# Low half of the second down weight tile of each feed-forward group: a VectorE subtraction in place of an accumulating DMA

## The chip, the cores and the metric

The kernel runs on one core of a Trainium2 chip. The metric is the device time of one execution in microseconds. The median of three runs before the change is 1435.9 us (1432.58 to 1439.35).

## The reference

One step of a hybrid decoder trunk of one layer, for a prompt of 1024 tokens and 8 sample sequences of 4 tokens that share the weights. What matters here is the second half of the layer:

```
h = x * (1 + scale2) + shift2
u = causal depthwise conv width 3 of (h @ w_up);  f = (silu(u_a) * u_b) @ w_down
x = LayerNorm(ALPHA * x + gate2 * f)
```

with `D_MODEL` 1024 and `D_FF` 2816, all in float32. Ahead of it stand the modulation, a combined projection, differential attention, a convolution branch, the output projection and a first LayerNorm.

## The kernel before

All 1056 tokens lie along the free dimension, in three chunks of 352 (`CH`). Features lie on the partitions. A float32 product is made of three matmuls in a 32-bit format of fewer bits (fp32r): each operand is split into a high half (a cast) and a low half (what the cast left), and `mm3` (lines 173 to 178) adds high x high (L176), high x low input (L177) and low weight x high input (L178) in PSUM.

**Weights.** They come as tiles of 128 x 1024 in the order of the list `wsrc` (lines 126 to 142). `prefetch_w` (lines 152 to 165) takes the next entry: SP loads it into `wst` (two buffers), ScalarE casts it into `whi` (L159), and the low half `wlo` is made in one of two ways, by the entry's second field `how`. With `"dma"`, ScalarE writes -hi into `wlo` (L161) and POOL issues a DMA that adds `wst` onto it in place (L162). With an engine, that engine subtracts (L164). `whi` and `wlo` have three buffers each, so a tile's cast waits until the matmuls of the tile three places earlier have ended.

**The feed-forward stage.** The 22 blocks of 128 features are worked off in groups of `FG` = 2, groups 0 to 10. A group has six weight tiles, in this order: for its first feature block the tiles of the two halves of `w_up` (called u1a, u1b here), the same for the second (u2a, u2b), then two tiles of `w_down` (d1, d2). For each block and chunk, `Up.chunk` (lines 1055 to 1086) makes two products into PSUM banks (`psb`, four in turn); ScalarE copies each out (L1062, L1063, L1065 for the sample columns of the last chunk), VectorE does the convolution taps (L1068, L1072), then SILU (L1078), the product (L1079), and the split into `ah` (L1080, ScalarE) and `al` (L1082, POOL). `down` (lines 1088 to 1094) then runs, chunk by chunk, eight blocks of six matmuls each: three with d1, three with d2. VectorE adds each block into the accumulator `acc` (L1179), which empties the bank.

Groups 1 to 9 make all low halves with `"dma"`; group 0 with VectorE. In group 10 the list `LAST` (line 44) sets the order: up and down for chunks 0 and 1 with `"dma"`, then the last chunk, whose tiles are loaded once more, with VectorE. `norm2` (lines 1096 to 1143) normalizes each chunk in three row tiles: statistics (L1116), a Newton iteration (L245 to L247), a scaling copy on ScalarE (L1134), an accumulating DMA of the bias (L1135) and the store (L1143), with four buffers `y`.

The order of instructions on each engine is set by a scheduler that runs its own timeline of the program, so that a change in one place can reorder others.

Of the kernel before, what the change touches and what calls it, by code (L numbers as in the profile page):

```python
# [36 lines left out]
FG = 2  # L37
# [31 lines left out]
def body(tc, nc, io):  # L69
    ex = ExitStack()  # L70
    with ex:
# [58 lines left out]
        for f0 in range(0, KF, FG):  # L130
            once = nc.vector if f0 // FG == CHUNK_OUTER[0] else "dma"

            def blocks(what, how):
                return [(io["w_up"][m], how) for f in range(f0, f0 + FG) for m in (f, KF + f)] if what == "u" else \
                    [(io["w_down"][f], how) for f in range(f0, f0 + FG)]

            if f0 + FG == KF:
                for w, cs in LAST:
                    if w != "n":
                        wsrc += blocks(w, "dma" if len(cs) > 1 else nc.vector)  # L140
            else:
                wsrc += blocks("u", once) * (NCH if f0 // FG in CHUNK_OUTER else 1) + blocks("d", once)
# [277 lines left out]
        with tc.tile_pool(name="pa", bufs=2, reuse_waits="tile") as pa:  # L420
# [19 lines left out]
            def flip_x(c):  # L440
                n = 4 if c < EARLY else 1
                for d0 in range(0, KD, n):
# [6 lines left out]
                    for j in range(n):  # L449
                        nc.scalar.copy(xs[c][:, d0 + j, :], ps[j][:, 0, :CH])  # L450

            blocks, loaded = [w + d for d in range(KD) for w in (0, 8)], []

            def load_ada():
# [830 lines left out]
```

## Time and profile before

| | us |
|---|---|
| median of the runs | 1435.9 (1432.58 to 1439.35) |
| the profiled execution | 1439.02 |
| its span | 1437.3 |
| busy: TensorE (PE) | 1356.3 |
| busy: VectorE (DVE) | 899.7 |
| busy: ScalarE (ACT) | 643.2 |
| busy: GpSimd (POOL) | 338.6 |
| mean granted TensorE clock, as a share | 0.975 |

Busy times are sums over one execution, taken by the hardware profiler. Matmuls are pipelined: one is recorded with some 0.32 us, the next starts 0.16 us after it, so a busy PE need not be at its peak. A line such as L178 is the line of the kernel that issued the instruction. "Idle before" is the time in which an engine stood still ahead of an instruction, with what ended it.

### The profile page before, as it was taken

The page shows a single profiled execution, that of the slowest core. Times are in us where ns is not written, and L with a number is a line of the kernel's source. Part 1 is how long each engine was busy: PE and PEld are TensorE (multiplying, and loading weights), DVE is VectorE, ACT ScalarE, POOL GpSimd, SP SyncE. Part 2 cuts the span into 40 slices and gives each one's busy share as a digit, 9 for nine tenths or more (in the row PEclk, how much of TensorE's full clock was granted, in tenths as well). Part 3 has the DMA queues.
Part 4 walks back from the last instruction along what each step waited for, and adds up shares of the span by engine and source line. Part 5 has one row for each costly group of instructions (what it writes and reads, how often), then busy time and mean ns, then how long its engine had stood idle before and what let it go on. Part 6 is the DMA issues. An engine that isn't in the chain of part 4 may idle for free.

```text
span 1437.3 us, 24575 instructions
## 1 busy us (share of the span) xinstructions
PE 1356.3 (94%) x9449; PEld 1271.1 (88%) x9449; DVE 899.7 (63%) x1954; ACT 643.2 (45%) x1170; POOL 338.6 (24%) x454
## 2 busy tenths in 40 slices
PE   7899999999999899789999999999999999999983
PEld 6798999996666798779999999999999999999983
DVE  5759999437777569987453545453536353535486
ACT  6542222457666455563434343435253525353532
POOL 2431110321101452324222122222222222221111
PEclk9999999999999999989999999999999999999996
DMA  9877666547764355432434243434242525252718
GB/s 302 283 214 218 185 186 192 148 130 272 239 224 166 115 173 166 123 97 76 100 78 105 72 88 90 93 84 105 72 113 65 118 60 117 59 118 60 190 57 208
DMA packets 71671, 199.68 MB, mean 139 GB/s; under 512 B 16002, under 2 KB 16514, under 8 KB 70658
## 3 DMA queue, kind: packets, MB, share of 16 engines
q1 hardware_dynamic: 57874, 145.55, 30.4%
q0 software_dynamic: 13680, 52.57, 18.8%
q8 instruction: 74, 1.21, 0.3%
q14 instruction: 43, 0.35, 0.1%
HBM read 137.49 MB, written 15.51 MB: 106 GB/s over the span
## 4 chain that ended last, share of the span: by engine, by line
PE 71%; DVE 10%; DMA 9%; issue 5%; ACT 3%; POOL 1%; SPq 0%; DVEq 0%; POOLq 0%; ACTq 0%
PE psb L176 20%; PE psb L178 20%; PE psb L177 19%; DMA wlo<-wst 6%; PE psa L836 4%; PE psb L877 2%; DVE wlo L164 2%; PE psa L319 1%; PE psb L753 1%; PE psb L866 1%; PE psb L788 1%; DMA y<-y 1%; DVE acc L1179 1%; DMA wada<-w_ada 1%; DVE t L1068 1%
## 5 line engine op out<-in xcount | busy, mean ns | idle before, releaser
L176 PE MATMUL psb<-h2h,whi 128*128 128x352 f32 x1056 | 343.1, 326 | 3.9 <-ACT h2h L294 3.9
L177 PE MATMUL psb<-h2l,whi 128*128 128x352 f32 x1056 | 341.1, 323 | 2.5 <-DVE h2l L295 2.5
L1068 DVE SCALAR_TENSOR_TENSOR t<-up,prm,t 128x352 f32<-128x352 f32 (+1 forms) x264 | 165.2, 627 | 282.9 <-ACT t L1063 280.0
L178 PE MATMUL psb<-h2h,wlo 128*128 128x352 f32 x1056 | 340.0, 325 | 0.6 <-DMA wlo<-wst 0.6
L159 ACT CAST whi<-wst 128x1024 fp32r<-128x1024 f32 x124 | 128.9, 1048 | 321.0 <-PE psb L177 283.3
L1179 DVE SCALAR_TENSOR_TENSOR acc<-psb,mod,acc 128x352 f32<-128x352 f32 (+1 forms) x288 | 160.4, 571 | 72.6 <-PE psb L178 66.7
L177 PEld LDWEIGHTS psb<-h2l,whi 128*128 128x128 f32 x1056 | 200.8, 190 | 3.3 <-DVE h2l L295 3.0
L176 PEld LDWEIGHTS psb<-h2h,whi 128*128 128x128 f32 x1056 | 199.7, 189 | 4.6 <-ACT h2h L294 4.2
L178 PEld LDWEIGHTS psb<-h2h,wlo 128*128 128x128 f32 x1056 | 199.7, 190 | 1.2 <-DMA wlo<-wst 1.2
L178 PE MATMUL psb<-ah,wlo 128*128 128x352 f32 x528 | 167.5, 327 | 8.9 <-DMA wlo<-wst 8.9
L176 PE MATMUL psb<-ah,whi 128*128 128x352 f32 x528 | 172.5, 329 | 2.7 <-DVE acc L1179 2.0
L177 PE MATMUL psb<-al,whi 128*128 128x352 f32 x528 | 172.0, 326 | 0.0
L178 PE MATMUL psb<-hh,wlo 128*128 128x352 f32 x480 | 157.0, 327 | 3.1 <-DMA wlo<-wst 3.1
L176 PE MATMUL psb<-hh,whi 128*128 128x352 f32 x480 | 158.1, 336 | 1.5 <-ACT sig L399 1.5
L177 PE MATMUL psb<-hl,whi 128*128 128x352 f32 x480 | 156.0, 326 | 0.0
L162 POOL DMA_DIRECT2D wlo<-wst x80 | 71.4, 893 | 343.3 <-ACT wlo L161 314.6
L375 DVE SCALAR_TENSOR_TENSOR cv<-u,prm,cv 128x1024 f32<-128x1024 f32 x120 | 151.3, 1296 | 0.8
L1082 POOL TENSOR_TENSOR al<-g,ah 128x352 fp32r<-128x352 f32 x60 | 60.6, 1010 | 251.8 <-ACT ah L1080 251.8
L178 PEld LDWEIGHTS psb<-ah,wlo 128*128 128x128 f32 x528 | 98.9, 190 | 11.8 <-DMA wlo<-wst 11.8
L176 PEld LDWEIGHTS psb<-ah,whi 128*128 128x128 f32 x528 | 100.2, 190 | 6.3 <-DVE acc L1179 5.0
L177 PEld LDWEIGHTS psb<-al,whi 128*128 128x128 f32 x528 | 100.5, 190 | 0.0
L1062 ACT COPY up<-psb 128x352 f32<-128x352 f32 (+1 forms) x132 | 58.4, 442 | 88.1 <-PE psb L178 88.0
(253 smaller groups left out, 2269.7 us busy)
## 6 DMA issues: line engine op xcount, KB each, us to landing
wlo<-wst POOLq DMA_DIRECT2D x80, 512.0 KB, 5.4
wst<-w_up SPq DMA_DIRECT2D x56, 512.0 KB, 3.7
wada<-w_ada SPq DMA_DIRECT2D x48, 512.0 KB, 5.3
kv<-kc SPq DMA_DIRECT2D x64, 256.0 KB, 5.4
kv<-vc SPq DMA_DIRECT2D x64, 256.0 KB, 4.6
wst<-w_out SPq DMA_DIRECT2D x24, 512.0 KB, 3.6
wst<-w_down SPq DMA_DIRECT2D x24, 512.0 KB, 4.2
wst<-w_in SPq DMA_DIRECT2D x20, 512.0 KB, 3.7
```

The costliest lines, as they stand in the source:

```text
L159: last_w["hi"] = nc.scalar.copy(hi, st)
L162: last_w["lo"] = nc.gpsimd.dma_start(lo.bitcast(F32), st, accum_op=ALU.add)
L164: last_w["lo"] = how.tensor_tensor(lo, st, hi.bitcast(F32), op=ALU.subtract)
L176: nc.tensor.matmul(ps, lhsT=wh, rhs=xh, start=start and i == 0, stop=False)
L177: nc.tensor.matmul(ps, lhsT=wh, rhs=xl, start=False, stop=False)
L178: nc.tensor.matmul(ps, lhsT=wl, rhs=xh, start=False, stop=stop and i == n - 1)
L375: nc.vector.scalar_tensor_tensor(acc, src, wj, acc, op0=ALU.mult, op1=ALU.add)
L836: nc.tensor.matmul(ps[m][:, i, :w], lhsT=q[r], rhs=k[r, i * w:(i + 1) * w], start=True, stop=True)
L1062: nc.scalar.copy(up[:, 2 + o:2 + o + npc], ps[:, 0, :npc])
L1068: nc.vector.scalar_tensor_tensor(t[:, :npc], up[:, o + j:o + j + npc], w, t[:, :npc], op0=ALU.mult, op1=ALU.add)
L1082: eng.tensor_tensor(self.al[:, c, :], g, self.ah[:, c, :].bitcast(F32), op=ALU.subtract)
L1179: nc.vector.scalar_tensor_tensor(x[:, :npc], ps[:, :npc], gate[:, 0:1], x[:, :npc], op0=ALU.mult, op1=ALU.add)
```

## The change

In every group, entries of `w_down` other than the group's first get `nc.vector` as their `how`.

```diff
             def blocks(what, how):
                 return [(io["w_up"][m], how) for f in range(f0, f0 + FG) for m in (f, KF + f)] if what == "u" else \
-                    [(io["w_down"][f], how) for f in range(f0, f0 + FG)]
+                    [(io["w_down"][f], how if f == f0 else nc.vector) for f in range(f0, f0 + FG)]
```

Ten tiles change: d2 of the groups 1 to 9, and d2 of group 10 for chunks 0 and 1. Group 0 and the last chunk had VectorE already. Each of the ten loses L161 on ScalarE and L162 on POOL's queue and gets L164 on VectorE. The scheduler moves other instructions with it.

The first place is TensorE at the start of a down phase (group 2; the other nine have the same pattern). `ah_8517` and `whi_8757` belong to the first feature block and d1, `ah_8527`, `whi_8969` and `wlo_8970` to the second and d2; `psb_8981`, `_8989`, `_8997`, `_9005` are the first four banks. Before, the rows of the fourth bank and what follows:

```order
L176 MATMUL psb_9005<-ah_8517,whi_8757 128x352
L177 MATMUL psb_9005<-al_8518,whi_8757 128x352
L178 MATMUL psb_9005<-ah_8517,wlo_8758 128x352
L176 MATMUL psb_9005<-ah_8527,whi_8969 128x352
L177 MATMUL psb_9005<-al_8528,whi_8969 128x352
L178 MATMUL psb_8981<-ah_8527,wlo_8970 128x352
L178 MATMUL psb_8989<-ah_8527,wlo_8970 128x352
L178 MATMUL psb_8997<-ah_8527,wlo_8970 128x352
L178 MATMUL psb_9005<-ah_8527,wlo_8970 128x352
L176 MATMUL psb_9013<-ah_8517,whi_8757 128x352
```

After the change, the first twelve rows of that phase (names are numbered anew; `wlo_8969` is d2's low half, `psb_8979` the first bank):

```order
L176 MATMUL psb_8979<-ah_8516,whi_8756 128x352
L177 MATMUL psb_8979<-al_8517,whi_8756 128x352
L178 MATMUL psb_8979<-ah_8516,wlo_8757 128x352
L176 MATMUL psb_8979<-ah_8526,whi_8968 128x352
L177 MATMUL psb_8979<-al_8527,whi_8968 128x352
L176 MATMUL psb_8987<-ah_8516,whi_8756 128x352
L177 MATMUL psb_8987<-al_8517,whi_8756 128x352
L178 MATMUL psb_8987<-ah_8516,wlo_8757 128x352
L176 MATMUL psb_8987<-ah_8526,whi_8968 128x352
L177 MATMUL psb_8987<-al_8527,whi_8968 128x352
L176 MATMUL psb_8995<-ah_8516,whi_8756 128x352
L178 MATMUL psb_8979<-ah_8526,wlo_8969 128x352
```

Before, the matmuls on d2's low half stood behind the 20 others of the first four banks. Now the first of them is the twelfth of the phase.

The second place is ScalarE and VectorE ahead of the same phase. ScalarE before, in group 2, from the cast of d2 (`whi_8969`) on; `psb_8892` is u2a's last product, `psb_8925` u2b's, `whi_8976` the next group's u1a:

```order
L159 CAST whi_8969<-wst_8967 128x1024
L1062 COPY up0_8519<-psb_8892 128x320
L1063 ACTIVATE t0_8917<-psb_8892,prm_73 128x352
L1065 COPY us0_8520<-psb_8892 128x8x4
L161 ACTIVATE wlo_8970<-whi_8969 128x1024
L1078 ACTIVATE g_8958<-t0_8917 128x352
L159 CAST whi_8976<-wst_8974 128x1024
L1062 COPY up1_8523<-psb_8925 128x320
```

ScalarE after:

```order
L159 CAST whi_8968<-wst_8966 128x1024
L1062 COPY up0_8518<-psb_8891 128x320
L1063 ACTIVATE t0_8916<-psb_8891,prm_73 128x352
L1065 COPY us0_8519<-psb_8891 128x8x4
L159 CAST whi_8974<-wst_8972 128x1024
L1078 ACTIVATE g_8957<-t0_8916 128x352
L1062 COPY up1_8522<-psb_8924 128x320
L1063 ACTIVATE t1_8949<-psb_8924,prm_73 128x352
```

VectorE in the same place of group 1, as a piece of the difference (`t_8229` is u2a's, `t_8262` u2b's last chunk):

```order
 L1079 TENSOR_TENSOR g<-g,t_8194 128x352
+L164 TENSOR_TENSOR wlo<-wst,whi 128x1024
 L1068 SCALAR_TENSOR_TENSOR t_8229<-up_7831,prm,t_8229 128x320
 L1072 SCALAR_TENSOR_TENSOR t_8229<-us_7832,prm,t_8229 128x32
 L1068 SCALAR_TENSOR_TENSOR t_8229<-up_7831,prm,t_8229 128x320
 L1072 SCALAR_TENSOR_TENSOR t_8229<-us_7832,prm,t_8229 128x32
+L1179 SCALAR_TENSOR_TENSOR acc_6133<-psb,mod,acc_6133 128x352 x2
 L1068 SCALAR_TENSOR_TENSOR t_8262<-up_7835,prm,t_8262 128x320
 L1072 SCALAR_TENSOR_TENSOR t_8262<-us_7836,prm,t_8262 128x32
+L1179 SCALAR_TENSOR_TENSOR acc_6133<-psb,mod,acc_6133 128x352
```

The negated copy is gone, the next group's first cast has moved ahead of the SILU, the subtraction stands ahead of u2a's last convolution step, and residual adds have come in ahead of and between u2b's convolution steps.

The third place is VectorE in the tail, where the reciprocal deviations of the first chunk's three row tiles are made (`nmt_14474`, `_14507`, `_14540` before; `nmt_14464`, `_14497`, `_14530` after). Before:

```order
L1079 TENSOR_TENSOR g_14734<-g_14734,t1_14726 128x352
L247 SCALAR_TENSOR_TENSOR nmt_14540<-nmt_14540 128x1
L245 SCALAR_TENSOR_TENSOR nmt_14507<-nmt_14507 128x1
L246 TENSOR_TENSOR nmt_14474<-nmt_14474 128x1
L1116 BN_STATS bn_14804<-psa_14793 128x6 x2
L245 SCALAR_TENSOR_TENSOR nmt_14540<-nmt_14540 128x1
L246 TENSOR_TENSOR nmt_14507<-nmt_14507 128x1
L247 SCALAR_TENSOR_TENSOR nmt_14474<-nmt_14474 128x1
L1082 TENSOR_TENSOR al_14032<-g_14734,ah_14031 128x352
```

After:

```order
L1079 TENSOR_TENSOR g_14724<-g_14724,t1_14716 128x352
L247 SCALAR_TENSOR_TENSOR nmt_14530<-nmt_14530 128x1
L246 TENSOR_TENSOR nmt_14464<-nmt_14464 128x1
L245 SCALAR_TENSOR_TENSOR nmt_14497<-nmt_14497 128x1
L245 SCALAR_TENSOR_TENSOR nmt_14530<-nmt_14530 128x1
L247 SCALAR_TENSOR_TENSOR nmt_14464<-nmt_14464 128x1
L246 TENSOR_TENSOR nmt_14497<-nmt_14497 128x1
L1116 BN_STATS bn_14794<-psa_14783 128x6
L246 TENSOR_TENSOR nmt_14530<-nmt_14530 128x1
L1116 BN_STATS bn_14794<-psa_14783 128x6
```

The last step of the first row tile (L247 on `nmt_14474`, now `nmt_14464`) stood behind the statistics of a later tile (L1116) and now stands ahead of them. On SP's queue the store of the fourth row tile now stands ahead of the third's.

## Rows read from the trace of the kernel before

**Rows 1.** The page, part 1: busy us, share of the span, instructions
```profile
PE 1356.3 (94%) x9449; PEld 1271.1 (88%) x9449; DVE 899.7 (63%) x1954; ACT 643.2 (45%) x1170; POOL 338.6 (24%) x454
```

**Rows 2.** The page, part 5: groups; busy, mean ns | idle before, what ended it
```profile
L178 PE MATMUL psb<-ah,wlo 128*128 128x352 f32 x528 | 167.5, 327 | 8.9 <-DMA wlo<-wst 8.9
L176 PE MATMUL psb<-ah,whi 128*128 128x352 f32 x528 | 172.5, 329 | 2.7 <-DVE acc L1179 2.0
```

**Rows 3.** Timeline, PE, group 5: start, us, instruction, [idle before <- releaser]
```profile
1018.58 0.32 PE L176 MATMUL psb<-ah,whi 128*128 128x352 f32 x1
...
1021.63 0.32 PE L177 MATMUL psb<-al,whi 128*128 128x352 f32 x1
1022.63 0.91 PE L178 MATMUL psb<-ah,wlo 128*128 128x352 f32 x4 [0.67 <-DMA wlo<-wst]
1023.74 0.43 PE L176 MATMUL psb<-ah,whi 128*128 128x352 f32 x1 [0.20 <-DVE acc L1179]
1024.01 0.32 PE L177 MATMUL psb<-al,whi 128*128 128x352 f32 x1
```

**Rows 4.** Timeline of the other engines around it, same columns
```profile
1014.56 0.95 POOL L1082 TENSOR_TENSOR al<-g,ah 128x352 fp32r<-128x352 f32 x1 [4.26 <-ACT ah L1080]
...
1014.77 1.05 ACT L159 CAST whi<-wst 128x1024 fp32r<-128x1024 f32 x1 [0.29 <-PE psb L177]
...
1016.65 1.08 ACT L161 ACTIVATE wlo<-whi 128x1024 fp32r<-128x1024 f32 x1
...
1016.73 0.55 DVE L1068 SCALAR_TENSOR_TENSOR t<-up,prm,t 128x320 f32<-128x320 f32 x1 [2.76 <-ACT t L1063]
...
1018.03 0.90 POOL L162 DMA_DIRECT2D wlo<-wst  x1 [0.63 <-DVE t L1068]
...
1018.18 0.50 ACT L1078 ACTIVATE g<-t 128x352 f32<-128x352 f32 x1 [0.45 <-DVE t L1072]
...
1018.61 1.05 ACT L159 CAST whi<-wst 128x1024 fp32r<-128x1024 f32 x1
...
1020.42 0.19 ACT L1065 COPY us<-psb 128x32 f32<-128x32 f32 x1
```

**Rows 5.** Timeline, PE: the waits of groups 1, 2 and 10, same columns
```profile
736.38 0.91 PE L178 MATMUL psb<-ah,wlo 128*128 128x352 f32 x4 [0.95 <-DMA wlo<-wst]
...
803.79 0.32 PE L176 MATMUL psb<-ah,whi 128*128 128x352 f32 x1
...
809.02 0.91 PE L178 MATMUL psb<-ah,wlo 128*128 128x352 f32 x4 [1.85 <-DMA wlo<-wst]
810.13 0.43 PE L176 MATMUL psb<-ah,whi 128*128 128x352 f32 x1 [0.20 <-DVE acc L1179]
...
1361.88 0.91 PE L178 MATMUL psb<-ah,wlo 128*128 128x352 f32 x4 [1.20 <-DMA wlo<-wst]
```

**Rows 6.** Windows: us, busy of PE, PEld, DVE, ACT, POOL, PEclk, DMA, GB/s
```profile
809.00:815.00 6.00, 5.79 (x25) 5.50 (x26) 3.79 (x8) 0.49 (x1) 0.94 (x1) 0.72 0.91 234
```

**Rows 7.** Line 164 on DVE: duration min/median/max in ns, first and last start
```profile
L164 DVE TENSOR_TENSOR wlo<-wst,whi x36: 1209/1220/1497, 524.1 to 1393.1; 128x1024 fp32r<-128x1024 f32 x36
```

**Rows 8.** The tail: timeline; DMA busy tenths from 1404 us; DMA issues, KB, landing
```profile
1401.10 1.30 DVE L1116 BATCH_NORM_STATS2 bn<-psa 128x6 f32<-128x512 f32 x2
...
1420.16 1.41 DVE L1131 SCALAR_TENSOR_TENSOR y<-psa,nmv,gb 128x512 f32<-128x512 f32 x2 [2.90 <-DMA y<-y]
...
1402.62 2.19 ACT L1134 ACTIVATE y<-y,nmt 128x1024 f32<-128x1024 f32 x2 [1.36 <-DVE nmt L247]
...
1404.07 0.89 POOL L1135 DMA_DIRECT2D y<-gb  x1 [9.00 <-ACT y L1134]
...
DMA  0389899989999999999999996999999950998300
...
y<-y SPq DMA_DIRECT2D x4, 512.0 KB, 6.2
```

**Rows 9.** Line 159 on ACT: idle us ahead of it, times, by releaser
```profile
  DMA wst<-w_up: 9.4, 7
```

## The prediction

> **What bounds the kernel now.** I read the page's busy times first, then PE's groups with the idle time ahead of them, then the timeline around one of those idle times, then the end of the span. TensorE is busy for 94% of the span [rows 1], so time can come back only where it waits or runs at its lower clock. In the feed-forward stage one wait repeats: the matmuls on the low half of a down weight stood idle for 8.9 us on `DMA wlo<-wst`, and the matmuls behind them for 2.0 us on the residual add of VectorE [rows 2]. The 8.9 us are ten waits, one in each of the groups 1 to 10: 0.95 us in the first, 1.85 in the second, 1.20 in the last [rows 5], 0.67 in group 5 [rows 3].
>
> The timeline of group 5 shows why [rows 3, 4]. I call the group's weight tiles u1a, u1b, u2a, u2b (up), d1, d2 (down). The high half of d2 can be cast only when PE has left u2a, whose buffer it takes: 1014.77, done by 1015.82. ScalarE then copies u2a's last result and makes the negated copy (L161) from 1016.65 to 1017.73; POOL issues the accumulating DMA at 1018.03; it lands in time for the matmul at 1022.63, 4.60 us after its issue. PE starts the down blocks at 1018.58. Its order already puts off the four matmuls that need the low half, until four PSUM banks are full; at 1021.79 it has nothing else to do and waits.
>
> **What one wait costs.** The recorded 0.67 us is less than the loss. Matmuls step by (1021.63 - 1018.58)/19 = 0.1605 us [rows 3], so the 25th of the down phase would start at 1018.58 + 24 x 0.1605 = 1022.43. It starts at 1023.74: 1.31 us lost, that is the recorded idle time and 0.64 us more (draining a pipeline whose matmuls last 0.32 us each, then 0.20 us for a bank that VectorE must empty first). The next step takes 0.27 us, 0.11 over the usual. In group 2 the down phase starts at 803.79 and its 25th matmul at 810.13 instead of 807.64, 2.49 us late with 1.85 recorded: again 0.64 more [rows 5]. For ten waits: 8.9 + 10 x 0.64 + 10 x 0.11 = **16.4 us**.
>
> After group 2's wait, the longest, the granted clock was 0.72 from 809 to 815 us, that is, PE ran part of that stretch at the lower of its two levels (1.2 for 2.4 GHz) [rows 6]. Lost: 6.00 x (1 - 0.72) = **1.7 us**. None of the other nine waits shows this. Without the wait nothing idles ahead of that stretch. Together **18.1 us**.
>
> **The change part by part.**
>
> *Removed.* Ten L161 copies of about 1.08 us on ScalarE [rows 4], which has slack, and ten accumulating DMAs of 512 KB with ten issues of 0.90 us on POOL. Nothing on POOL's queue behind that issue is urgent: next come the memset and state copy for the next group and the DMA of the next u1a, which PE needs only after the 144 down matmuls, 23 us on.
>
> *Added.* Ten subtractions on VectorE. The same operation on the same shape ran 36 times, 1.209 to 1.497 us, median 1.220 [rows 7]; I take the median. VectorE's order puts it ahead of u2a's last convolution step. VectorE idled 2.76 us before that step [rows 4], so it is free when the cast ends at 1015.82; the low half is ready at about 1015.9 + 1.22 = 1017.1. PE's new order needs it at the 12th down matmul, 1018.58 + 11 x 0.1605 = 1020.35: 3.2 us of slack. The convolution step moves from 1016.73 to about 1017.1, and its result feeds the third chunk of the down phase, 15 us later. So the sum charges nothing for the subtraction; the cover is that VectorE gap, and if it were gone the cost would begin only past 3.2 us. With the low half in time, banks are finished one by one, so the 0.20 us wait on VectorE goes too.
>
> *Moved on ScalarE.* The cast of the next u1a now stands ahead of the SILU of u2a's chunk (L1078) and of the copies of u2b's last result. The SILU, 0.43 us from its start to the next [rows 4], thus comes between the cast and those copies, and u2b's bank comes free at about 1020.61 + 0.43 = 1021.04. The fourth down block needs that bank at its first matmul, the 19th: 1018.58 + 18 x 0.1605 = 1021.47. Cost zero, with 0.43 us to spare; this is the tightest margin that I find.
>
> *Moved on VectorE.* Two residual adds now stand ahead of u2b's convolution step. They wait for banks that PE closes at the 12th and 13th down matmul, about 1020.7 and 1020.9, just when the copies on ScalarE end for which that step waits anyway. It slips by about 1 us, and the third chunk covers that.
>
> *Moved on SP's queue.* The load of the next u1b waits for d2's staging buffer. That is free when the subtraction ends rather than when the DMA lands, some 5.5 us earlier; PE uses the tile after the down phase, so nothing is gained or lost.
>
> A rule of the Trainium skill speaks against the subtraction ("SBUF — State Buffer", section "Who interferes with whom"): a VectorE instruction with two inputs in SBUF and a GpSimd instruction that reads SBUF exclude each other, the second waiting for the whole of the first. The rows show little of it: over 36 runs the subtraction was never longer than 1.497 us. By the rule it could sit behind the POOL operation at 1014.56 (0.95 us), which is over before the cast ends, or behind the small POOL copies after it. What it would take to matter is rival 3 below.
>
> *The tail.* From about 1405 us on, the core's DMA engines are almost full until 1431 [rows 8]: six accumulating DMAs add the last bias to the output, and buffers wait for output stores (1420.16). The scheduler has reordered this tail. The first output tile's scale now leaves VectorE ahead of the statistics at 1401.10 instead of behind them, so its copy on ScalarE, at 1402.62 before, can start at about 1401.3, and the first accumulating DMA at about 1402.7 instead of 1404.07. The second tile's copy now stands behind a table load and gains nothing. The fourth tile's store overtakes the third's. A full DMA stage that starts 1.3 us sooner ends about that much sooner: **1.3 us** gained. Bounds: 2.5 us gained, if the DMAs behind it close up as well; 4.9 us lost, if one buffer waits for a whole extra 512 KB transfer (6.2 us median [rows 8], less the 1.3). I take 1.3 as nearest to the row that moved.
>
> **The sum.** The profiled execution took 1439.0 us (span 1437.3). 1439.0 - 18.1 - 1.3 = 1419.6. The median of the runs is 1435.9, 3.1 us lower. If what sets the profiled execution apart is the long wait of group 2 and its clock drop (2.49 - 1.31 + 1.7 = 2.9 us), a median run loses only 18.1 - 2.9 = 15.2, and 1435.9 - 15.2 - 1.3 = 1419.4. Both ways meet; if the median run had the full loss, it would be 1416.5. I predict **1419 us**.
>
> **The rivals.**
> 1. *Only the recorded idle comes back.* PE's pipeline might recover the 0.64 us elsewhere: 1439.0 - 8.9 - 2.0 = 1428.1. Against it: the step count above gives the same 0.64 in two groups. Chance 0.08.
> 2. *The tail eats part of it.* The stage is bound by DMA there, and the swapped stores delay a buffer: 1439.0 - 18.1 + 4.9 = 1425.8. For it: stores already hold VectorE up in the trace. Chance 0.10.
> 3. *The subtraction is late, or the change moves nothing.* If VectorE and POOL block each other as in the rule above, the subtraction must lose more than 3.2 us to hold PE at all, three POOL operations of 0.95 us and more. Then the wait is back and the time stays near 1434 to 1437. The order shows the DMAs gone, so "it does nothing" has no other way in. Chance 0.05.
> 4. *Slower.* The cast of the next u1a is now ahead of u2b's copies, so whatever holds the cast holds a PSUM bank. It waits for PE's last read of u2b, as before, and for its staged load. With a lateness L of the cast, each group loses L - 0.43 us; past L = 0.43 + 1.81 = 2.24 us the ten groups lose more than the 18.1 us gained. ScalarE did wait for up loads seven times, 9.4 us in all [rows 9], a mean of 1.3; at 3 us in every group the time would be 1439.0 - 18.1 + 25.7 = 1446.6. Against it: the cast at 1018.61 had no idle time recorded ahead of it [rows 4], so its load was there. Chance 0.05.
>
> **How the numbers follow.** My forecast has 0.72, with a range of its own of 1414 to 1424: from both sums with the 2.5 us tail bound and some spread of runs below, to a tail without gain and group waits that leave a few us above. Up to rival 2 the range becomes **1413 to 1426**, which leaves out rivals 1, 3 and 4 (0.18). About 0.5%, 7.2 us, is what a measurement of this kernel can tell from no change, so faster means below 1428.7. Faster: 0.72 + 0.10 + 0.06 of rival 1 = 0.88. Same: 0.02 + 0.05 = 0.07. Slower: 0.05.
>
> **What would show each step.** Right: the group of matmuls on the down weights' low half falls from 8.9 us of idle time to under 1; ten more L164 subtractions at about 1.22 us; L161 and L162 at 70 instead of 80; groups 69.3 us apart instead of 70.7; no clock below 1.00 between 740 and 1350. Wrong: a new PE wait on a PSUM bank (for a copy on ScalarE) at the fourth down block; L164 at 2 us or more; a last third of the tail in which output buffers wait longer than now.

## The result, and the profile after

Three runs of the changed kernel took 1414.04, 1417.65 and 1425.17 us, median **1417.65 us** against 1435.9 before: a ratio of 0.9862, 95% interval 0.9826 to 0.9898. The forecast was 1419 us, 1413 to 1426. The profiled execution took 1414.04 us, with a span of 1412.3.

To see where the time went, I cut the span of each profiled execution at two points that every version has. The first is the wait of TensorE for the first low input of the feed-forward stage (L177, `h2l`), before any changed instruction. Here it is before:

```profile
645.30 0.66 PE L177 MATMUL psb<-h2l,whi 128*128 128x352 f32 x1 [2.54 <-DVE h2l L295]
```

and after:

```profile
639.74 0.66 PE L177 MATMUL psb<-h2l,whi 128*128 128x352 f32 x1 [3.14 <-DVE h2l L295]
```

The second is the 25th down matmul of group 10 for chunks 0 and 1, where the last changed tile has been used: at 1362.98 before, 1339.22 after. I call what lies ahead of the first point the start, between them the stage, behind them the tail.

| us | start | stage | tail | span |
|---|---|---|---|---|
| before | 645.30 | 717.68 | 74.32 | 1437.3 |
| after | 639.74 | 699.48 | 73.08 | 1412.3 |
| difference | 5.56 | **18.20** | 1.24 | 25.0 |

The stage lost 18.2 us, where 18.1 were forecast, and the tail 1.24, where 1.3 were. The 5.56 us of the start are ahead of the change. The experiments show how much that part moves by itself: in the ten of them that leave it alone it took 642.0 to 651.3 us.

The busy times, to be read beside [rows 1], and the groups that answer to [rows 2]:

```profile
PE 1342.0 (95%) x9449; PEld 1264.6 (90%) x9449; DVE 909.9 (64%) x1964; ACT 632.0 (45%) x1160; POOL 331.9 (24%) x444
...
L176 PE MATMUL psb<-ah,whi 128*128 128x352 f32 x528 | 170.7, 326 | 0.8 <-ACT ah L1080 0.8
...
L178 PE MATMUL psb<-ah,wlo 128*128 128x352 f32 x528 | 169.1, 324 | 0.0
```

VectorE has ten instructions more, ScalarE and GpSimd ten fewer each. The 8.9 us ahead of L178 on a down weight are gone altogether, and so are the 2.0 us on the residual add ahead of L176.

Group 5's down phase on TensorE, to be read beside [rows 3] (start, us, instruction): the rows of its first, 12th, 19th and 25th matmul.

```profile
1004.09 0.32 PE L176 MATMUL psb<-ah,whi 128*128 128x352 f32 x1
...
1005.87 0.48 PE L178 MATMUL psb<-ah,wlo 128*128 128x352 f32 x2
...
1007.00 0.32 PE L176 MATMUL psb<-ah,whi 128*128 128x352 f32 x1
...
1007.96 0.32 PE L176 MATMUL psb<-ah,whi 128*128 128x352 f32 x1
```

From the first to the 25th it is 3.87 us, 5.16 before. Over the groups 1 to 10 this stretch summed to 53.75 us before and 38.64 after: 15.1 us, against 8.9 + 6.4 = 15.3 in the forecast.

The other engines around it, to be read beside [rows 4]:

```profile
1000.29 1.05 ACT L159 CAST whi<-wst 128x1024 fp32r<-128x1024 f32 x1 [0.29 <-PE psb L177]
...
1001.37 1.22 DVE L164 TENSOR_TENSOR wlo<-wst,whi 128x1024 fp32r<-128x1024 f32 x1 [1.89 <-ACT whi L159]
1002.51 0.55 DVE L1068 SCALAR_TENSOR_TENSOR t<-up,prm,t 128x320 f32<-128x320 f32 x1
...
1001.75 0.93 POOL L1085 TENSOR_SCALAR fst<-up 128x2 f32<-128x2 f32 x1 [0.72 <-ACT up L1062]
...
1004.13 1.05 ACT L159 CAST whi<-wst 128x1024 fp32r<-128x1024 f32 x1 [1.84 <-PE psb L177]
1005.08 0.49 ACT L1078 ACTIVATE g<-t 128x352 f32<-128x352 f32 x1
...
1006.33 0.19 ACT L1065 COPY us<-psb 128x32 f32<-128x32 f32 x1
```

The subtraction starts when the cast of d2 ends, takes 1.22 us and is over at 1002.59, 1.5 us before the down phase and 3.3 us before the matmul that needs it. The copies of u2b's product end at 1006.52, 2.43 us after the phase's start; the fourth block's first matmul, the 19th, stands at 2.91.

Windows of the same length as [rows 6] around group 2's down phase, and of the groups 3 to 9:

```profile
796.00:802.00 6.00, 6.00 (x40) 6.00 (x38) 3.64 (x9) 3.34 (x6) 1.99 (x7) 1.00 0.35 106
802.00:808.00 6.00, 6.00 (x40) 6.00 (x39) 4.05 (x9) 0.49 (x1) 0.95 (x1) 1.00 0.67 153
871.00:1330.00 459.00, 458.96 (x2862) 458.67 (x2861) 237.17 (x527) 185.75 (x332) 96.46 (x167) 1.00 0.37 86
```

The granted clock is 1.00 where it was 0.72, and for 459 us TensorE is busy in all but 0.04.

### The profile page after: what moved, and what is told of

Its sections match the earlier page's. It is cut to its first block, busy times and chain, and to the rows that moved or that the text cites. A ratio compares the mean times of both kernels' runs of the same rounds, so it can differ in the third digit from the quotient of the medians.

```text
span 1412.3 us, 24553 instructions
## 1 busy us (share of the span) xinstructions
PE 1342.0 (95%) x9449; PEld 1264.6 (90%) x9449; DVE 909.9 (64%) x1964; ACT 632.0 (45%) x1160; POOL 331.9 (24%) x444
## 4 chain that ended last, share of the span: by engine, by line
PE 78%; DVE 9%; DMA 5%; ACT 3%; issue 3%; SPq 0%; POOL 0%; DVEq 0%; POOLq 0%; ACTq 0%
PE psb L176 22%; PE psb L178 22%; PE psb L177 21%; PE psa L836 4%; PE psb L877 2%; DMA wlo<-wst 2%; DVE wlo L164 2%; PE psa L319 1%; PE psb L866 1%; PE psb L788 1%; PE psb L753 1%; DMA y<-y 1%; DMA y<-gb 1%; DVE t L1068 1%; DVE h2l L295 1%
## 5 line engine op out<-in xcount | busy, mean ns | idle before, releaser
L176 PE MATMUL psb<-h2h,whi 128*128 128x352 f32 x1056 | 342.1, 325 | 4.0 <-ACT h2h L294 4.0
L177 PE MATMUL psb<-h2l,whi 128*128 128x352 f32 x1056 | 340.4, 322 | 3.1 <-DVE h2l L295 3.1
L178 PE MATMUL psb<-h2h,wlo 128*128 128x352 f32 x1056 | 339.3, 324 | 0.5 <-DMA wlo<-wst 0.4
L177 PEld LDWEIGHTS psb<-h2l,whi 128*128 128x128 f32 x1056 | 200.4, 190 | 3.8 <-DVE h2l L295 3.4
L176 PEld LDWEIGHTS psb<-h2h,whi 128*128 128x128 f32 x1056 | 199.0, 189 | 4.6 <-ACT h2h L294 4.3
L178 PEld LDWEIGHTS psb<-h2h,wlo 128*128 128x128 f32 x1056 | 199.0, 189 | 1.1 <-DMA wlo<-wst 1.1
L176 PE MATMUL psb<-ah,whi 128*128 128x352 f32 x528 | 170.7, 326 | 0.8 <-ACT ah L1080 0.8
L177 PE MATMUL psb<-al,whi 128*128 128x352 f32 x528 | 171.3, 324 | 0.0
L178 PE MATMUL psb<-ah,wlo 128*128 128x352 f32 x528 | 169.1, 324 | 0.0
L178 PE MATMUL psb<-hh,wlo 128*128 128x352 f32 x480 | 156.8, 327 | 3.1 <-DMA wlo<-wst 3.1
L176 PE MATMUL psb<-hh,whi 128*128 128x352 f32 x480 | 157.9, 336 | 1.5 <-ACT sig L399 1.5
L177 PE MATMUL psb<-hl,whi 128*128 128x352 f32 x480 | 155.8, 325 | 0.0
L162 POOL DMA_DIRECT2D wlo<-wst x70 | 62.4, 898 | 316.5 <-ACT wlo L161 300.4
L1082 POOL TENSOR_TENSOR al<-g,ah 128x352 fp32r<-128x352 f32 x60 | 60.3, 1004 | 245.5 <-ACT ah L1080 245.5
L176 PEld LDWEIGHTS psb<-ah,whi 128*128 128x128 f32 x528 | 99.5, 189 | 1.6 <-ACT ah L1080 1.0
L177 PEld LDWEIGHTS psb<-al,whi 128*128 128x128 f32 x528 | 99.9, 189 | 0.0
L178 PEld LDWEIGHTS psb<-ah,wlo 128*128 128x128 f32 x528 | 99.5, 189 | 0.0
```

The costliest lines, as they stand in the source:

```text
L162: last_w["lo"] = nc.gpsimd.dma_start(lo.bitcast(F32), st, accum_op=ALU.add)
L176: nc.tensor.matmul(ps, lhsT=wh, rhs=xh, start=start and i == 0, stop=False)
L177: nc.tensor.matmul(ps, lhsT=wh, rhs=xl, start=False, stop=False)
L178: nc.tensor.matmul(ps, lhsT=wl, rhs=xh, start=False, stop=stop and i == n - 1)
L1082: eng.tensor_tensor(self.al[:, c, :], g, self.ah[:, c, :].bitcast(F32), op=ALU.subtract)
```

## Experiments

All of them start from the changed kernel; the diffs show its lines with a minus. In the table the ratio is to runs of the kernel before on the same chip (medians 1439 to 1440 us there); `again` is the change itself, repeated.

| kernel | median us | ratio (95%) | start | stage | tail |
|---|---|---|---|---|---|
| d1 instead of d2 | 1440.48 | 1.0012 (0.9996 to 1.0027) | 647.94 | 717.22 | 73.84 |
| d2 by GpSimd | 1427.41 | 0.9913 (0.9887 to 0.9940) | 645.47 | 709.00 | 72.53 |
| subtracted twice | 1424.48 | 0.9902 (0.9873 to 0.9931) | 642.00 | 700.11 | 72.19 |
| groups 1 to 5 | 1429.00 | 0.9929 (0.9907 to 0.9951) | 645.95 | 708.56 | 72.09 |
| both down tiles | 1418.62 | 0.9861 (0.9833 to 0.9890) | 651.30 | 700.04 | 72.26 |
| u2b copied 2 times | 1421.60 (one run) | | 647.86 | 700.53 | 71.41 |
| u2b copied 4 times | 1423.13 (one run) | | 649.56 | 700.34 | 71.50 |
| bias on VectorE | 1424.06 | 0.9897 (0.9878 to 0.9917) | 649.83 | 700.07 | 72.50 |
| again | 1421.86 | 0.9870 (0.9850 to 0.9890) | 649.42 | 700.86 | 72.82 |
| bias on GpSimd | 1422.92 | 0.9878 (0.9859 to 0.9898) | 646.67 | 700.20 | 74.73 |
| first four weights | 1413.13 | 0.9808 (0.9786 to 0.9829) | 641.32 | 699.50 | 73.18 |
| first eight weights | 1409.82 | 0.9793 (0.9769 to 0.9817) | 638.84 | 700.07 | 72.69 |

Two executions of the changed kernel differ by 1.4 us in the stage (699.48 and 700.86), so in that column one us is nothing, while 8 or 17 are. I judge theories on the stage by it rather than by medians, in which the start varies more.

### The other down tile

```diff
-                    [(io["w_down"][f], how if f == f0 else nc.vector) for f in range(f0, f0 + FG)]
+                    [(io["w_down"][f], nc.vector if f == f0 else how) for f in range(f0, f0 + FG)]
```

> The same exchange on the other down tile: in groups 1 to 9 and in group 10 for chunks 0 and 1 the low half of d1 is made by VectorE, that of d2 again by the accumulating DMA. ScalarE loses the same ten L161, POOL's queue the same ten DMAs, VectorE gets the same ten subtractions as in the change. Theory A (the gain is the ten waits of TensorE on d2's low half): d1's low half was never waited for, so nothing is gained; the ten waits stay, some 8 to 9 us of idle time ahead of the L178 matmuls on a down weight, the feed-forward stage stays near 717 us, the time near 1434. Rival B (the gain comes from less work on ScalarE, POOL and the DMA engines, whichever tile it is taken from): stage near 700 us, time near 1418. Rival C, between them: with one 512 KB DMA less in flight, d2's DMA lands sooner, and half of the waiting goes: stage near 709 us, time near 1427.

The group of matmuls on a down weight's low half, group 2's wait, and a window that begins just ahead of it:

```profile
L178 PE MATMUL psb<-ah,wlo 128*128 128x352 f32 x528 | 166.9, 326 | 8.7 <-DMA wlo<-wst 8.7
...
811.74 1.28 PE L178 MATMUL psb<-ah,wlo 128*128 128x352 f32 x4 [1.90 <-DMA wlo<-wst]
...
809.00:815.00 6.00, 4.10 (x17) 3.52 (x16) 3.28 (x8) 0.93 (x2) 2.04 (x5) 0.76 0.84 169
```

The same work was taken off the same engines, and nothing was gained: 8.7 us of waiting, a stage of 717.22 us. Rivals B and C fall. What the change gains is the wait for d2, not the load that it takes away. Group 2's long wait is there again, and the low granted clock after it too.

### Both down tiles

```diff
-                    [(io["w_down"][f], how if f == f0 else nc.vector) for f in range(f0, f0 + FG)]
+                    [(io["w_down"][f], nc.vector) for f in range(f0, f0 + FG)]
```

> The low halves of both down tiles, d1 and d2, are made by VectorE in the ten places; TensorE's order stays that of the change. Theory A (only a half that TensorE waits for is worth anything): d1's was never late, so nothing more is gained; stage 699 to 700 us, time near 1420 where the kernel before takes 1438 to 1440. Rival B (each accumulating DMA less is worth something, through ScalarE, POOL's queue or the DMA engines): another part of the gain, stage below 697 us. Rival C (VectorE runs out of room or gets into the way of u2a's convolution steps): stage above 702 us.

The stage is 700.04 us, and the ratio the change's own. Theory A again: d1's half was never late. Nor does VectorE run out of room.

### Half of the groups

```diff
-                    [(io["w_down"][f], how if f == f0 else nc.vector) for f in range(f0, f0 + FG)]
+                    [(io["w_down"][f], how if f == f0 or f0 // FG > 5 else nc.vector) for f in range(f0, f0 + FG)]
```

> The change in the groups 1 to 5 alone; groups 6 to 10 make d2's low half with the accumulating DMA as before. Theory A (each wait costs its recorded idle time and 0.75 us, and the drop of the clock after group 2's wait 1.7 us): the groups 1 to 5 held about 4.8 us of the recorded idle time, so 4.8 + 5 x 0.75 + 1.7 = 10.2 us of the 18.1 come back: stage near 707.5 us, time near 1427, five waits left, and no clock below 1.00 near group 2. Rival B (only the recorded idle time comes back): 4.8 us, stage near 713 us. Rival C (the clock drop is not tied to group 2's wait): it shows again in a profile in which group 2 has no wait, stage near 709 us.

The stage is 708.56 us: 9.1 of the 18.2 us came back. The waits of groups 6 and 7, and the window behind the latter:

```profile
1084.34 0.91 PE L178 MATMUL psb<-ah,wlo 128*128 128x352 f32 x4 [1.18 <-DMA wlo<-wst]
...
1156.10 0.91 PE L178 MATMUL psb<-ah,wlo 128*128 128x352 f32 x4 [1.58 <-DMA wlo<-wst]
...
1158.00:1164.00 6.00, 6.00 (x39) 6.00 (x38) 4.38 (x9) 0.49 (x1) 0.95 (x1) 1.00 0.63 187
```

Five waits are left, of 5.5 us in all, where the same five groups held some 4.1 before. That is 1.4 us more, and the gain is 1.1 us short of the forecast for it, so the longer waits account for the shortfall; why they grew, no run shows. Rival B, that only recorded idle time comes back, falls: in the groups 1 to 5 the stretch of 24 steps fell from 27.2 us to 19.3, by 7.9, with 4.8 recorded. Rival C falls as well: the clock near group 2 stayed at 1.00. The wait of 1.58 us was not followed by a lower clock; those of 1.85 [rows 5] and 1.90 us were.

### Twice the subtraction

```diff
-                    [(io["w_down"][f], how if f == f0 else nc.vector) for f in range(f0, f0 + FG)]
+                    [(io["w_down"][f], how if f == f0 or how != "dma" else "twice") for f in range(f0, f0 + FG)]
...
-                    last_w["lo"] = how.tensor_tensor(lo, st, hi.bitcast(F32), op=ALU.subtract)
+                    last_w["lo"] = [(nc.vector if how == "twice" else how).tensor_tensor(lo, st, hi.bitcast(F32), op=ALU.subtract) for _ in range(1 + (how == "twice"))][-1]
```

> The change with each of the ten subtractions done twice by VectorE, one after the other, into the same tile (the result is the same). Theory A (the subtraction is hidden, with some 3.2 us between its end and the first matmul that needs it): 1.22 us more in ten places cost nothing; VectorE is busy some 12 us longer, the stage stays near 700 us, the time near 1418. Rival B (VectorE's time is on the path, through the convolution steps and residual adds that stand behind the subtraction): 0.3 to 1.2 us per group, stage 703 to 712 us, time 1421 to 1430.

Group 5, whose down phase starts at 1007.08:

```profile
1004.36 1.22 DVE L164 TENSOR_TENSOR wlo<-wst,whi 128x1024 fp32r<-128x1024 f32 x1 [1.89 <-ACT whi L159]
1005.50 0.55 DVE L1068 SCALAR_TENSOR_TENSOR t<-up,prm,t 128x320 f32<-128x320 f32 x1
1005.97 0.24 DVE L1072 SCALAR_TENSOR_TENSOR t<-us,prm,t 128x32 f32<-128x32 f32 x1
1006.13 1.22 DVE L164 TENSOR_TENSOR wlo<-wst,whi 128x1024 fp32r<-128x1024 f32 x1
```

The half is ready at 1007.35, 0.27 us into the phase where it was 1.50 ahead of it in the change, and convolution steps are pushed back too; the stage is 700.11 us, with no wait. Charging nothing for the subtraction was right, and it would have been right for twice as much.

### The subtraction on GpSimd

```diff
-                    [(io["w_down"][f], how if f == f0 else nc.vector) for f in range(f0, f0 + FG)]
+                    [(io["w_down"][f], how if f == f0 or how != "dma" else nc.gpsimd) for f in range(f0, f0 + FG)]
```

> d2's low half is subtracted by GpSimd instead of VectorE, in the same ten places; the rest of the change stays. GpSimd's subtractions of this shape took 2.35 to 3.07 us in group 0. Theory A (only the moment counts at which the low half is ready): the cast ends about 2.8 us before the down phase starts, so the half is ready about 0.4 us before that start and needed no sooner than the twelfth matmul, 1.8 us after it; no wait, stage near 700 us, time near 1418. Rival B (it matters that it is VectorE: GpSimd's queue, with its memset, its split of the second chunk and its DMA issues, gets the tile late, or the two engines hold each other up while both read SBUF): waits on the low half of 0.3 to 1 us per group, stage 705 to 715 us, time 1423 to 1432.

The stage is 709.00 us, half of the gain lost. Group 5, whose down phase starts at 1014.19 (TensorE's 16th and 19th matmul first, then GpSimd, VectorE and ScalarE):

```profile
1016.61 0.64 PE L178 MATMUL psb<-ah,wlo 128*128 128x352 f32 x3
1017.59 0.43 PE L176 MATMUL psb<-ah,whi 128*128 128x352 f32 x1 [0.34 <-ACT us L1065]
...
1011.51 2.40 POOL L164 TENSOR_TENSOR wlo<-wst,whi 128x1024 fp32r<-128x1024 f32 x1 [0.39 <-ACT whi L159]
...
1012.34 1.92 DVE L1068 SCALAR_TENSOR_TENSOR t<-up,prm,t 128x320 f32<-128x320 f32 x1 [2.76 <-ACT t L1063]
...
1014.80 0.24 DVE L1072 SCALAR_TENSOR_TENSOR t<-us,prm,t 128x32 f32<-128x32 f32 x1
...
1015.16 0.50 ACT L1078 ACTIVATE g<-t 128x352 f32<-128x352 f32 x1 [2.78 <-POOL up L1048]
1015.57 1.03 ACT L159 CAST whi<-wst 128x1024 fp32r<-128x1024 f32 x1
...
1017.36 0.18 ACT L1065 COPY us<-psb 128x32 f32<-128x32 f32 x1
```

Theory A was right on the low half itself: it is ready at 1013.91, and no matmul waits for it. But u2a's convolution step, 0.55 us in the change, lasted 1.92 us and ended at 1014.26, 0.35 us after GpSimd's subtraction. Three more short steps on the same tile follow, the last of them over at 1015.04, and the SILU starts 0.12 us after that, as it started 0.11 us after its last step in the kernel before (its row names a small memset of GpSimd, L1048, which ended at 1015.10; the SILU reads nothing of it). The cast stands behind the SILU, and u2b's copies behind the cast: these end 3.35 us after the phase's start instead of 2.43. The fourth block wants that bank at 2.89 and waits. In nine groups TensorE stood idle for 0.34 us, recorded on the copies (L1065, 3.0 us in all), and each group lost 70.13 - 69.29 = 0.84 us. The 1.37 us that the step lost are more than the 0.46 by which the bank is late, so without them the wait would go, by this count; no run took the overlap away with GpSimd kept.

The longer step is not the whole cause. In the change the cast stands ahead of the SILU (1004.13 and 1005.08); in this version the scheduler put it behind (1015.57 and 1015.16). In the order of the change, I estimate, the cast could have started when TensorE left u2b, just after 1014.19, and u2b's copies would have ended some 2.4 us into the phase as they did there, in time. By this count the wait needs both, the slow step and this order, and no run parted them: what is shown is that this version loses half of the gain, not that GpSimd must. Rival B's size is right, its place is not. Its text takes the 2.35 to 3.07 us from group 0; the rows are those of the output projection (470.9 to 520.2 us before), and the size held: 2.40 us here.

The rule of the Trainium skill that the prediction weighed ("SBUF — State Buffer", section "Who interferes with whom") fits these rows: the VectorE step with two inputs in SBUF finished only after the whole of GpSimd's instruction. The change meets it the other way round, where it costs nothing: GpSimd's small copy (L1085), 0.22 us before beside an idle VectorE, took 0.93 us from 1001.75 on and ended 0.09 us after the subtraction. Nothing waits for that copy.

### How tight is u2b's bank

```diff
-                        nc.scalar.copy(up[:, 2 + o:2 + o + npc], ps[:, 0, :npc])
+                        for _ in range(4 if i and c == NCH - 1 and self.f % FG and 0 < self.f // FG < 10 else 1): nc.scalar.copy(up[:, 2 + o:2 + o + npc], ps[:, 0, :npc])
```

and the same with 2 for 4.

> The change, with the copy of u2b's product in its last chunk (L1062, 128x320) done twice by ScalarE in the groups 1 to 9, into the same place. It holds the PSUM bank which the fourth down block needs. In the profile of the change that bank is free 2.43 us after the start of the down phase and wanted at 2.89 us, by the same count of matmuls as in the prediction: some 0.4 us to spare. One more copy takes 0.31 us. Theory A (this margin is real, and nothing else is as tight): no wait, stage 699.5 to 700.5 us. Rival B (the margin is used up otherwise): a wait on ScalarE's copy in each group, stage 702 to 706 us.

> As the one with two copies, but with four: 0.93 us more on ScalarE in front of the bank's release, in nine groups. Theory A (margin of 0.4 us): the bank is 0.5 us late, as it was where GpSimd made the subtraction, and costs what it did there, 0.84 us per group: TensorE waits some 0.35 us on ScalarE's copy in nine groups, stage near 707 us. Rival B (the margin is far larger than counted, since the scheduler or the pipeline absorbs it): no wait, stage below 701 us. Rival C (each group loses the whole 0.93 us): stage near 708.5 us.

Neither made TensorE wait: stages of 700.53 and 700.34 us. ScalarE with four copies, in the group whose down phase starts at 1014.78, and TensorE's 19th matmul:

```profile
1016.17 0.41 ACT L1062 COPY up<-psb 128x320 f32<-128x320 f32 x1
1016.48 1.06 ACT L161 ACTIVATE wlo<-whi 128x1024 fp32r<-128x1024 f32 x1
1017.44 1.33 ACT L1062 COPY up<-psb 128x320 f32<-128x320 f32 x3
...
1019.21 0.19 ACT L1065 COPY us<-psb 128x32 f32<-128x32 f32 x1
...
1017.70 0.32 PE L176 MATMUL psb<-ah,whi 128*128 128x352 f32 x1
```

u2b's bank is free only at 1019.40, yet the 19th matmul runs at 1017.70. The scheduler had given the fourth block another bank: here that matmul waits for VectorE's residual add of an earlier block, which was over 2.7 us after the phase's start, in the change for ScalarE's copy. With two copies it waits for VectorE too. Rival B of the second run came in, and the two runs say nothing on the size of the margin. They do say that my step "the fourth block needs u2b's bank" is not a property of the kernel: the scheduler decides it anew for each version.

### The tail without accumulating DMAs

```diff
-                    if not last:
+                    if not c:
                         nc.scalar.activation(y, y, AF.Copy, scale=r)
...
-                        if last:
+                        if c:
                             nc.vector.scalar_tensor_tensor(y[:, j, :], y[:, j, :], r, gb[:, 1, j * 512:j * 512 + 512],
```

> The change, and in the tail the second chunk's output bias is added by VectorE together with the scale (as in the last chunk) instead of by three accumulating DMAs of 512 KB. Theory A (the tail is bound by its DMAs, and VectorE waits there for buffers): three DMAs of six go, 3 to 6 us are gained, the tail goes from 73.1 to 67 to 70 us. Rival B (VectorE, 88% busy there, becomes the bound: three tiles x 1.40 us more on it): nothing gained or 1 to 4 us lost.

```diff
-                        nc.gpsimd.dma_start(y, gb[:, 1, :].rearrange("p (i w) -> p i w", i=2), accum_op=ALU.add)
+                        nc.gpsimd.tensor_tensor(y, y, gb[:, 1, :].rearrange("p (i w) -> p i w", i=2), op=ALU.add)
```

> The change, and in the tail the output bias of the first and second chunk is added by GpSimd (an addition in SBUF) instead of by six accumulating DMAs of 512 KB. GpSimd idles there for all but the issues. Theory A (the tail is bound by its DMAs): the six are replaced by six additions of 2.4 to 3.1 us on an engine that is free, buffers come back sooner, the tail goes from 73 to 68 to 71 us, and the time is 2 to 5 us under the change alone. Rival B (the tail is bound by the chain through the last chunk's down products and statistics, as the exchange to VectorE suggested, where the tail stayed at 72.5 us): within 1.5 us of the change. Rival C (GpSimd's additions hold up VectorE's operations on SBUF, as was seen when GpSimd made the subtraction): slower by 2 to 6 us.

The last 20 us of the change:

```profile
1392.00:1412.00 20.00, 2.18 (x9) 1.78 (x9) 13.14 (x32) 2.96 (x5) 1.71 (x2) 0.50 0.83 240
```

of the version with VectorE:

```profile
1402.00:1422.00 20.00, 2.20 (x8) 1.43 (x8) 16.06 (x41) 0.78 (x3) 0.00 (x0) 0.59 0.44 151
```

and of that with GpSimd:

```profile
1401.00:1421.00 20.00, 4.22 (x23) 3.16 (x21) 16.82 (x43) 3.07 (x5) 4.71 (x2) 0.59 0.34 119
```

The DMA engines fell from 0.83 busy to 0.44 and 0.34, and the tail did not get shorter: 72.50 and 74.73 us against 73.08 and 72.82. VectorE fills up instead: 16.06 and 16.82 us of 20, where it had 13.14. In time neither is better than the change (ratios 0.9897 and 0.9878, 0.9870 for the change repeated; the version with GpSimd 1.06 us above it on the same chip). The gain that Theory A forecast did not come in either version.

Its mechanism did, though. VectorE stood idle for 5.8 us in the tail of the change repeated until output buffers came back (L1131 on `DMA y<-y`), for 1.6 us in the version with VectorE and not at all in that with GpSimd. What was given back there went to VectorE. In the first version it adds the bias of three more tiles (L1138, 8.5 us instead of 4.1). That is Rival B. In the second, GpSimd's additions held it up, as Rival C said (GpSimd first, then VectorE, then a matmul that waited for it):

```profile
1386.00 2.37 POOL L1135 TENSOR_TENSOR y<-y,gb 128x1024 f32<-128x1024 f32 x1 [6.83 <-ACT y L1134]
1388.64 2.38 POOL L1135 TENSOR_TENSOR y<-y,gb 128x1024 f32<-128x1024 f32 x1 [0.27 <-ACT y L1134]
...
1386.03 2.71 DVE L1082 TENSOR_TENSOR al<-g,ah 128x352 fp32r<-128x352 f32 x1
1388.67 2.36 DVE L247 SCALAR_TENSOR_TENSOR nmt<-nmt 128x1 f32<-128x1 f32 x1
...
1388.80 0.43 PE L177 MATMUL psb<-al,whi 128*128 128x352 f32 x1 [1.82 <-DVE al L1082]
```

In the change repeated the same two VectorE steps took 0.52 and 0.15 us. Over the last 42 us three kinds of step (L1082, L247, L1185), as many in both, took 13.1 us instead of 3.5. So part of VectorE's busy time there is waiting and not work. By its time this version falls under Rival B (within 1.5 us), but what its rows show is Rival C's hold-up, at a lower price than Rival C gave. Neither version took work from the DMA engines without burdening VectorE, so what the tail would be with fewer DMAs alone, no run shows.

### The same exchange where the weights begin

```diff
-            wsrc += [(io["w_in"][m], "dma") for m in ((16 + i, 12 + i) if w == "g" else (4 * "qkv".index(w) + i, ))]
+            wsrc += [(io["w_in"][m], nc.vector if len(wsrc) < 4 else "dma") for m in ((16 + i, 12 + i) if w == "g" else (4 * "qkv".index(w) + i, ))]
```

and the same with 8 for 4.

> The change itself once more, on the chip of the two other kernels of this call, so that they have it beside them. Every theory: the ratio to the kernel before near 0.986, stage near 700 us; the start up to the feed-forward stage varies by several us from run to run.

> The change, and the same exchange in another place where TensorE waits for the low half of a weight: the first four tiles of the input projection (near 30 us, where the DMA engines are full) get VectorE instead of the accumulating DMA. In the profile of the change the two waits there were 1.50 and 1.62 us. Theory A (the lesson carries over): with 0.64 us more for each as in the feed-forward stage, some 3 to 4.5 us less than the change alone; no wait on a low half before 100 us. Rival B (the start is bound by its DMAs, so TensorE will wait for the next load instead): within 1.5 us of the change. Rival C (VectorE is needed there for the normalization of the input, and the subtractions of 1.22 us get ahead of it): slower by 1 to 5 us.

> As the kernel with VectorE for the first four tiles of the input projection, now for the first eight. There TensorE has no wait on a low half left, and the kernel ran at 0.981 of the kernel before, 8.7 us under the change alone, of which 3 to 4.5 us were the waits that the change's profile shows. Theory A (beyond the waits, each accumulating DMA that is not moved while the DMA engines are full is worth something; they are full up to 50 us and 70 to 80% busy after): tiles five to eight, used from 80 to 110 us, give little, 0 to 3 us more: time 1410 to 1413 where the kernel before takes 1440. Rival B (it is four DMAs' worth at any place): 4 to 9 us more, 1404 to 1409. Rival C (VectorE, 94% busy between 100 and 150 us, loses by it): 1 to 5 us slower than with four.

With four tiles the median is 1413.13 us, 8.7 under the change on the same chip, about twice what Theory A gave; rivals B and C fall. The window from 30 to 40 us and a wait in it, in the change repeated:

```profile
30.00:40.00 10.00, 7.13 (x60) 6.19 (x59) 6.00 (x20) 2.99 (x8) 3.81 (x5) 0.83 1.04 360
...
35.93 0.65 PE L319 MATMUL psa<-wada,csil 128*32 128x128 f32 x16 [2.87 <-DMA wada<-w_ada]
```

and the window with the first four tiles on VectorE:

```profile
30.00:40.00 10.00, 10.00 (x87) 6.76 (x80) 8.40 (x25) 2.76 (x8) 3.41 (x4) 1.00 0.88 342
```

TensorE is busy throughout, at full clock, where it waited for a load of the modulation's weights; between these two profiles the start is 8.1 us shorter. The gain itself rests on the times: five runs of 1409.98 to 1415.72 us against five of 1419.72 to 1424.82. For its cause there is one profile of each, and the first profile of the change had both waits on a low half (1.50 and 1.62 us) and still a start of 639.74 us, shorter than the 641.32 here. In the repeated change TensorE did not wait for a low half there at all (0.0 us on `hh,wlo`, 3.1 in the first profile of it); it waited for other loads. So between these two profiles the mechanism that I gave, the two waits on a low half, is not what paid. The DMA engines, full in that window and no longer so, point to the transfers themselves as the price, but no run separated the two. With eight tiles the ratio is 0.9793 (0.9769 to 0.9817): the fastest version of the study, though not to be told from the one with four. That is Theory A of the last run, little more from four tiles used after the DMA engines' full stretch.

## Why the prediction was right

**What bounds.** Right. The waits for d2's low half carried the gain: exchange d1 and nothing moves, exchange both and nothing is added, and half of the groups gives half.

**The price of a wait.** Recorded idle time, 0.64 us for the pipeline and the bank, 0.11 for the next step: 16.4 us, with 15.1 measured in the stretches of 24 steps against 15.3 forecast for them. From one group's 25th down matmul to the next group's it went from the usual 70.70 to 69.29 us. Rival 1 would have left the stage 11 us shorter, not 18.2.

**The clock.** 1.7 us were forecast for the low clock after group 2's wait. From group 2's 25th down matmul to group 3's it took 72.22 us before, 1.5 more than the usual 70.70. The low clock is gone in the change and in the version with the groups 1 to 5, and there again where the wait is (d1 instead of d2). Stage less stretches is 18.2 - 15.1 = 3.1 us; the 1.1 of the next steps and the 1.7 make 2.8.

**The subtraction.** 1.22 us, ready 1.5 us ahead of the down phase, as forecast, and 3.3 us of slack for the 3.2 forecast. The doubled subtraction shows that the cover is real. Rival 3 did not come in: the longest of the 46 subtractions took 1.498 us, and their overlap with GpSimd lengthened GpSimd's copies.

**The margin on ScalarE.** For the change itself right: no wait, with 0.48 us between the bank and the matmul (0.43 forecast). The version with GpSimd shows that past this margin TensorE waits where I said, and each group lost 0.84 us, though there with the cast behind the SILU, an order that I had not counted with. That a fixed bank is behind it was wrong: the scheduler can pick another, and did in the two versions with repeated copies. Rival 4's own cause, a late load for the cast, did not occur: ScalarE's waits for up loads (9.1 us after, 9.4 before) fell on casts outside the ten places.

**The tail.** 1.24 us for 1.3, so rival 2, a longer tail, did not come in. The first step of the reasoning came as written. This is the issue of the first accumulating DMA after the change:

```profile
1378.79 0.91 POOL L1135 DMA_DIRECT2D y<-gb  x1 [7.57 <-ACT y L1134]
```

It stands 39.57 us behind the start of the tail, where the one before (1404.07, [rows 8]) stood at 41.09: 1.5 us sooner, for the 1.4 forecast. VectorE's waits for output buffers fell from 7.1 to 5.9 us. In d1 instead of d2 that DMA came 0.5 us sooner than before, and the tail was 0.5 us shorter. The exact size is worth little all the same. The changed kernel and the versions whose tail I left alone took 71.4 to 73.2 us, the kernel before and d1 instead of d2 74.3 and 73.8: a gain of about that size is likely, its exact value is not shown. Nor is the reason for the rest, that the end follows because the stage is full of DMAs: the two versions with fewer DMAs had no shorter tail, but both loaded VectorE in exchange.

**What I left out.** The start. The sum was made against one execution, 1439.02 us, and I laid its distance from the median to group 2's wait. The start alone varies by 12 us between profiled executions, more than that distance; my second way to the same 1419 was therefore no confirmation. Nor is the long wait in group 2 peculiar to that execution: d1 instead of d2 has it again (1.90 us) in a profile of 1440.73 us, beside a median of 1440.48. What the prediction got right is the 19.4 us of stage and tail; that the median came out within 1.4 us of 1419 is in part luck, with runs from 1414.04 to 1425.17 us.

## What to carry to other kernels

In a stage that TensorE bounds, an exchange of engines was worth what TensorE waited for its result, not the work that it moved (at the start, where the DMA engines are full, it was worth more than the waits seen): look for the one tile of a group whose half arrives last, and add to the recorded idle time what the pipeline loses around it (here 0.64 + 0.11 us a wait). Before putting it on another engine, look at what runs beside it there: the same subtraction was free on VectorE and came with the loss of half of the gain on GpSimd, through a slowed convolution step and an order that the scheduler had changed. Where a scheduler writes the order, a margin counted in one version is a fact of that version.

## What was not expected of the hardware

GpSimd and VectorE kept each other out over whole instructions: a step of 0.55 us on VectorE took 1.92 beside GpSimd's subtraction of 2.40, a copy of 0.22 us on GpSimd 0.93 beside VectorE's of 1.22, and in the tail a step of 0.15 us on VectorE took 2.36 beside GpSimd's addition of 2.38. Such a step counts as busy, so a profile shows VectorE at work where it waits. In the rows before the change I had taken the effect for small. And the first 640 us, with much the same program, took 639.7 to 651.3 us from one profiled execution to the next; in `again` (649.4 us) the granted clock was 0.90 in the first 50 us, in the profile after (639.7 us) it was 1.00.
